# Seven block products in three feed-forwards: weight sums on VectorE, down products in small groups between the pairs

## The chip, the cores and the metric

The kernel runs on one core of a Trainium2 chip. The core has TensorE (PE in the profile) for matrix products, which writes to PSUM, eight banks of 128 x 512 numbers; VectorE (DVE) and ScalarE (ACT), which work on PSUM and on the on-chip memory SBUF; SyncE (SP), which here only issues the DMA transfers; and GpSimd (POOL), which this kernel hardly uses. The engines run their own queues of instructions in order and wait for each other with semaphores. The metric is the time of one execution on the device in microseconds.

## What is computed

Three layers in a row, on 528 rows (16 learned and 512 given) of width 1024, in 32-bit floats: a mixer and a feed-forward, a second mixer and a feed-forward, and then a third mixer and feed-forward on the 512 given rows. The change touches the feed-forwards alone:

```python
def conv_ffn(h, w_up, w_gate, conv_w, conv_b, w_down):      # layers 1 and 2
    u = h @ w_up                                            # 1024 -> 2816
    g = h @ w_gate
    g = lax.conv_general_dilated(g, conv_w...) + conv_b     # 3 taps along the rows, each column alone
    return (jax.nn.silu(g) * u) @ w_down                    # 2816 -> 1024
...
h = h + conv_ffn(rmsnorm(h, norm_ffn[l]), ...)
...
act = silu(rms_norm(x) @ w_gate) * (rms_norm(x) @ w_up)     # layer 3, no convolution
x = x + act @ w_down
```

## The kernel before

**Layout.** Numbers are kept transposed: `hT[k]` holds 128 of the 1024 columns on the partitions and the 528 rows along the free side. The hidden width 2816 is 22 tiles `f` of 128. A weight tile is `[128, 1024]`: the 8 blocks of 128 x 128 that one output tile needs.

**Precision.** Each 32-bit operand is split in two rounded halves, high and low (`w_hi`, `w_lo` of a weight; `xh`, `xl` of the layer's input; `ah`, `al` of the activations), and a product is three matmuls: high by high, high by low, low by high. The high half is a cast, and the low half a subtraction on VectorE. In `split` the cast is recorded by `O.copy`, which the planner may put on ScalarE or VectorE; a plain `SC.copy` stays on ScalarE.

**The first two feed-forwards** are `ffn(0, 1)` and `ffn(1, 3)`, called ffn0 and ffn1 below. For each `f`, `gate_up(f)` multiplies the gate tile over all eight `k`, `8 x 3` matmuls for each range of columns (two of 264 in ffn0; two of 258 in ffn1), reads the banks with the row scale `r` into `g`, runs the convolution as one ScalarE and two VectorE passes into `y`, takes the silu, multiplies the up tile (two ranges of 264; in ffn1 one of 512) into `y` and splits it into `ah`, `al`. `down(gi)` multiplies the down weights of a group of `f` (`GROUPS`: 8, 8 and 6 of them) for the eight output tiles `m`, and adds each bank to `hT[m]`. It stands in the program behind the first `f` of the next group.

**The third feed-forward** (`block2_ffn`, ffn2 below) does without the convolution, on 512 columns. From `f = FS = 2` on it multiplies gate and up together, as a 2 x 2 matrix of blocks by Winograd's seven products instead of eight (`gate_up_fast`). The halves of a weight pair are summed on VectorE into `s13` and `s24` and split there and on ScalarE (`weights`); the sums of the input (`th`, `tl`) are made once. Each product is 4 blocks x 3 matmuls on 256 columns. `sp` and `sv` hold intermediate sums read from the banks, `u` the up result.

**What sets the order.** Every operation is recorded, and at the end of a stage `flush` plans it: a list scheduler with a cost for each instruction, a rank for each stage (`RANK`) and the true dependences, those of reused buffers among them. Weights are recorded with a priority 500 places earlier (`O.shift -= 500`). What it emits is fixed; on the chip each engine takes its own list in order. The profile names one line, L493, for all of it, since one helper emits every instruction; so the rows are told apart by tile names. Weight buffers: three each of `w_raw`, `w_hi`, `w_lo`, and in ffn2 two more of each (`s_raw`, `s_hi`, `s_lo`), taken round by `Ring`. PSUM banks are `d` (three), `at` (four) and `pv` (one); `AllBanks` deals out `d` and `at`.

Of the kernel before, what the change touches and what calls it, by code (L numbers as in the profile page):

```python
# [11 lines left out]
F32 = mybir.dt.float32  # L12
# [16 lines left out]
GROUPS = ((0, 8), (8, 16), (16, 22))  # L29
# [14 lines left out]
FS = 2  # L44
HS = S // 2
# [144 lines left out]
def prepare(i):  # L190
# [23 lines left out]
    for n, (f0, f1) in enumerate(GROUPS):  # L214
# [370 lines left out]
def body(ctx: ExitStack, tc, A, out):  # L585
# [18 lines left out]
    class AllBanks:  # L604
# [514 lines left out]

    def ffn(l, n):  # L1120
# [6 lines left out]
        with ExitStack() as es:  # L1127
# [600 lines left out]
    def block2_ffn():  # L1728
        with ExitStack() as es:
# [6 lines left out]
            class Ring:  # L1736


                def __init__(self, dt, *places):
                    self.dt, self.places, self.n = dt, places, 0  # L1740

                def tile(self):
                    pl, name, bufs = self.places[self.n % len(self.places)]
                    self.n += 1
                    return pl.tile([P, D], self.dt, name=name, bufs=bufs)

            ring = lambda dt, a, b: Ring(dt, *((wp, a, 3), (fp, b, 2)) * 2, (wp, a, 3))
            raws, his, los = ring(F32, "w_raw", "s_raw"), ring(F32R, "w_hi", "s_hi"), ring(F32R, "w_lo", "s_lo")

            def early(fn):  # L1750
                O.shift -= 500
                v = fn()
                O.shift += 500
                return v

            def halves(raw, hi=None, lo=None):

                n = raw.shape[1]
                hi = his.tile()[:, :n] if hi is None else hi
                lo = los.tile()[:, :n] if lo is None else lo  # L1760
# [125 lines left out]
```

## Time and profile before

| | us |
|---|---|
| median of 3 runs | 2363.95 (2362.64 to 2364.92) |
| the profiled execution | 2365.07 |
| its span, first to last instruction | 2362.9 |
| TensorE busy in the span | 2334.1 (99%) |
| VectorE busy | 1793.0 (76%) |
| ScalarE busy | 968.3 (41%) |

Busy time is the time that an engine's records cover. Records of one engine may overlap, so that their durations add up to more than the busy time. A row of groups gives the operation, what it writes and reads, its shape and its count; then the time that the group covers and the mean of one record; then the time that the engine stood idle before these instructions, and what ended it. TensorE's matmul records overlap most, and the time of one in a row is best read from a stretch with nothing else in it, as the stretch's time by the count.

### The profile page before, as it was taken

The numbers are of one execution on the slowest core, as the hardware profiler recorded it, in microseconds if no ns is written. First come the engines' busy times: TensorE is split into PE (matmuls) and PEld (weight loads), VectorE is DVE, ScalarE is ACT, GpSimd is POOL, SyncE is SP. The second block draws the span as 40 slices with busy tenths as digits, with TensorE's granted clock in tenths as the row PEclk, the third lists the DMA queues.
The fourth block names the chain that finished last, engine by engine and source line by source line (L and its number), as shares of the span: only waits on it lengthen the run. The fifth ranks groups of instructions, "written<-read, shape, count | busy, mean of one in ns | idle before, by whom it ended". The sixth has DMA issues, their size and how long they took to land.

```text
span 2362.9 us, 38568 instructions
## 1 busy us (share of the span) xinstructions
PE 2334.1 (99%) x15488; PEld 2125.5 (90%) x15488; DVE 1793.0 (76%) x3512; ACT 968.3 (41%) x1842; POOL 0.2 (0%) x4
## 2 busy tenths in 40 slices
PE   7999999999999999999999999999999999999999
PEld 7999999999999999999888888877888888889998
DVE  6999898764655779997665647876898877987965
ACT  4423556310111278885211203344677613443422
POOL 0000000000000000000000000000000000000000
PEclk9999999999999999999999999999999999999999
DMA  5222221322222211103223223322222122332322
GB/s 200 70 72 70 73 84 57 111 92 90 90 90 88 93 64 55 55 25 102 90 90 100 90 90 97 122 70 86 82 90 72 53 95 89 102 122 80 126 77 84
DMA packets 66546, 205.98 MB, mean 87 GB/s; under 512 B 7972, under 2 KB 14576, under 8 KB 66368
## 3 DMA queue, kind: packets, MB, share of 16 engines
q1 hardware_dynamic: 66368, 203.53, 27.1%
q8 instruction: 121, 1.98, 0.4%
q14 instruction: 57, 0.47, 0.1%
HBM read 201.37 MB, written 6.84 MB: 88 GB/s over the span
## 4 chain that ended last, share of the span: by engine, by line
PE 94%; DVE 3%; DMA 2%; issue 1%; ACT 1%; SPq 0%; DVEq 0%; ACTq 0%
PE d L493 54%; PE at L493 37%; PE pv L493 2%; DMA w_raw<-w_even 1%; DVE w_lo L493 1%; DVE s_lo L493 1%; DVE w_raw L493 0%; DMA w_raw<-w_gs 0%; DVE g L493 0%; DMA h<-h 0%; ACT w_hi L493 0%; DMA ob<-c_oh 0%; DVE sqh L493 0%; DVE s_raw L493 0%; SPq L493 0%
## 5 line engine op out<-in xcount | busy, mean ns | idle before, releaser
L493 PE MATMUL d<-xh,w_hi 128*128 128x264 f32 (+5 forms) x2082 | 616.2, 318 | 8.1 <-ACT w_hi L493 8.0
L493 PE MATMUL d<-xl,w_hi 128*128 128x264 f32 (+5 forms) x2082 | 618.4, 319 | 1.1 <-DVE xl L493 1.0
L493 PE MATMUL d<-xh,w_lo 128*128 128x264 f32 (+5 forms) x2082 | 614.0, 318 | 0.0
L493 DVE TENSOR_TENSOR w_lo<-w_raw,w_hi 128x1024 fp32r<-128x1024 f32 (+4 forms) x363 | 401.1, 1107 | 53.2 <-PE d L493 18.4
L493 PEld LDWEIGHTS d<-xh,w_hi 128*128 128x128 f32 x2082 | 377.4, 189 | 36.3 <-ACT w_hi L493 8.0
L493 PEld LDWEIGHTS d<-xl,w_hi 128*128 128x128 f32 x2082 | 377.3, 189 | 25.9 <-DVE xl L493 2.3
L493 PEld LDWEIGHTS d<-xh,w_lo 128*128 128x128 f32 x2082 | 376.3, 189 | 26.6 <-issue 1.9
L493 ACT CAST w_hi<-w_raw 128x1024 fp32r<-128x1024 f32 (+5 forms) x181 | 172.8, 955 | 328.2 <-PE d L493 230.5
L493 DVE CAST w_hi<-w_raw 128x1024 fp32r<-128x1024 f32 (+4 forms) x182 | 116.4, 640 | 188.0 <-PE d L493 113.0
L493 PE MATMUL at<-xh,w_hi 128*128 128x264 f32 (+3 forms) x822 | 240.1, 302 | 1.2 <-DVE h L493 1.2
L493 PE MATMUL at<-xh,w_lo 128*128 128x264 f32 (+3 forms) x822 | 240.1, 302 | 0.0
L493 PE MATMUL at<-xl,w_hi 128*128 128x264 f32 (+3 forms) x822 | 240.1, 302 | 0.0
L493 ACT ACTIVATE y<-g,cp 128x528 f32<-128x528 f32 (+1 forms) x44 | 36.2, 824 | 345.6 <-DVE g L493 345.6
L493 PEld LDWEIGHTS at<-xh,w_hi 128*128 128x128 f32 x822 | 152.8, 189 | 7.5 <-issue 1.6
L493 PEld LDWEIGHTS at<-xh,w_lo 128*128 128x128 f32 x822 | 152.8, 189 | 5.4
L493 PEld LDWEIGHTS at<-xl,w_hi 128*128 128x128 f32 x822 | 152.6, 189 | 5.2
L493 PE MATMUL at<-ah,w_lo 128*128 128x264 f32 (+1 forms) x350 | 113.0, 331 | 0.0
L493 PE MATMUL at<-ah,w_hi 128*128 128x264 f32 (+1 forms) x350 | 113.0, 332 | 0.0
L493 PE MATMUL at<-al,w_hi 128*128 128x264 f32 (+1 forms) x350 | 112.9, 332 | 0.0
L493 PE MATMUL d<-ah,w_hi 128*128 128x264 f32 (+1 forms) x274 | 91.1, 333 | 0.0
L493 PE MATMUL d<-al,w_hi 128*128 128x264 f32 (+1 forms) x274 | 91.0, 332 | 0.0
L493 PE MATMUL d<-ah,w_lo 128*128 128x264 f32 (+1 forms) x274 | 90.7, 332 | 0.0
(604 smaller groups left out, 4849.9 us busy)
## 6 DMA issues: line engine op xcount, KB each, us to landing
w_raw<-w_gu SPq DMA_DIRECT2D x92, 512.0 KB, 3.7
w_raw<-w SPq DMA_DIRECT2D x59, 512.0 KB, 3.6
w_raw<-w_dn SPq DMA_DIRECT2D x42, 512.0 KB, 3.8
w_raw<-w_even SPq DMA_DIRECT2D x41, 512.0 KB, 3.8
w_raw<-w_gs SPq DMA_DIRECT2D x25, 512.0 KB, 3.6
w_raw<-w_odd SPq DMA_DIRECT2D x24, 512.0 KB, 3.5
w_raw<-w_dn SPq DMA_DIRECT2D x21, 384.0 KB, 3.1
s_raw<-w_gs SPq DMA_DIRECT2D x15, 512.0 KB, 3.6
```

Source lines behind the costliest of these rows:

```text
L493: return f(*[r(x) for x in a], **{n: r(x) for n, x in k.items()})
```

## The change

Winograd's seven products, which only ffn2 had, are moved into a class `Fast` that all three feed-forwards use. In ffn0 and ffn1 the first two `f` stay as they were, `WHOLE` names three more (6, 11, 16) that keep all eight products (their weights come from the paired tiles through `Fast.tile`), and 17 `f` go through `Fast.pair`. Since two halves of 264 or 258 columns do not fit one bank there, a pair takes four banks in ffn0 and ffn1, three in ffn2. All casts of the weights in `Fast` are `SC.copy`. The convolution is unchanged, and `y` is then multiplied by `u`. Down groups become 4, 4, 4, 4, 3, 3 tiles in ffn0 and ffn1 and 5, 5, 5, 4, 3 in ffn2, and the eight `m` of a group are spread over the `f` of the next one. Buffers: `y` 3 to 2, `ah` and `al` 10 to 8 in ffn0 and ffn1; the halves of the seventh weight block (`s_hi2`, `s_lo2`) one each there, two in ffn2. `AllBanks` deals out `pv` too.

```diff
-GROUPS = ((0, 8), (8, 16), (16, 22))
+GROUPS = ((0, 4), (4, 8), (8, 12), (12, 16), (16, 19), (19, 22))
+GROUPS2 = ((0, 5), (5, 10), (10, 15), (15, 19), (19, 22))
+WHOLE = ((6, 11, 16), (6, 11, 16), ())
...
-            return (pd, pp, pd, pp, pd, pp, pp)[AllBanks.turn % 7].tile(shape, dt, name=("d", "at", "d", "at", "d", "at", "at")[AllBanks.turn % 7])
+            pl, place = ((pd, "d"), (pp, "at"), (pd, "d"), (pp, "at"), (pd, "d"), (pp, "at"), (pp, "at"), (pq, "pv"))[AllBanks.turn % 8]
+            return pl.tile(shape, dt, name=place)
...
+        def halves(self, raw, hi=None, lo=None):
...
+            SC.copy(hi, raw)
+            V.tensor_tensor(lo, raw, hi.bitcast(F32), op=ALU.subtract)
...
+        def blocks(self, f):
+            i = f - FS
+            r1, r2 = self.load(A[self.name][2 * i]), self.load(A[self.name][2 * i + 1])
+            s13, s24 = self.raws.tile(), self.raws.tile()
+            two = lambda t: t.rearrange("p (a b) -> p a b", a=2)
+            V.tensor_tensor(two(s13), two(r2)[:, 0:1, :].to_broadcast([P, 2, 512]), two(r1), op=ALU.add)
+            V.tensor_tensor(s24[:, :512], s13[:, :512], r1[:, 512:], op=ALU.add)
+            V.tensor_tensor(s24[:, 512:], s24[:, :512], r2[:, 512:], op=ALU.add)
+            w1, w24, w13 = self.halves(r1), self.halves(s24), self.halves(s13)
+            a12 = self.halves(r2[:, 512:], *(self.fp.tile([P, 512], F32R, name=n, bufs=self.small_bufs) for n in ("s_hi2", "s_lo2")))
+            part = lambda w, i: tuple(v[:, 4 * i:4 * i + 4, :] for v in w)
+            return part(w1, 1), a12, part(w1, 0), part(w13, 0), part(w24, 0), part(w13, 1), part(w24, 1)
...
+        def pair(self, f, g, u, r):
...
+            self.times(c11, a11, self.b[0][0], True)
+            SC.copy(p, c11)
+            self.times(q, s2, self.t[1], True)
+            self.times(q2, s3, self.t[2], True)
+            V.tensor_tensor(v, q, p, op=ALU.subtract)
+            V.tensor_tensor(p, q2, v, op=ALU.add)
+            self.times(s_, s1, self.t[0], True)
+            V.tensor_tensor(u[:, w:2 * w], p, s_, op=ALU.subtract)
+            self.times(c11, a12, self.b[1][0], False)
+            V.tensor_tensor(g[:, :w], c11, r[:, :w], op=ALU.mult)
+            self.times(q2, a22, self.t[3], False)
+            V.tensor_tensor(u[:, :w], q2, v, op=ALU.add)
+            self.times(s_, s4, self.b[1][1], False)
+            V.tensor_tensor(v, s_, v, op=ALU.subtract)
+            V.tensor_tensor(g[:, w:2 * w], v, r[:, w:2 * w], op=ALU.mult)
...
             def gate_up(f):
                 g = fp.tile([P, gw + 2], F32, name="g")
                 V.memset(g[:, 0:2], 0.0)
-                proj(pall, wtile(f"w_gu{l}", 2 * f), x, times(g[:, 2:], r), grange)
-                y = fp.tile([P, uw], F32, name="y", bufs=3)
+                if f < FS:
+                    proj(pall, wtile(f"w_gu{l}", 2 * f), x, times(g[:, 2:], r), grange)
+                elif f in WHOLE[l]:
+                    fast.tile(f, 0, times(g[:, 2:], r), x, grange)
+                else:
+                    u = fp.tile([P, gw], F32, name="u", bufs=1)
+                    fast.pair(f, g[:, 2:], u, r)
+                y = fp.tile([P, uw], F32, name="y", bufs=2)
...
-                proj(pall, wtile(f"w_gu{l}", 2 * f + 1), xu, times(y, y), urange)
-                acts[f] = split_new(y, fp, "ah", "al", 10, uw)
...
+                else:
+                    V.tensor_tensor(y, u[:, o:], y, op=ALU.mult)
+                acts[f] = split_new(y, fp, "ah", "al", 8, uw)
...
-                for m in range(KD):
-                    proj(pall, wtile(f"w_dn{l}_{gi}", m, f1 - f0), a, add_h(m, u0), urange)
-                    if gi == 2:
+                for m in ms:
+                    w = early(lambda: fast.halves(fast.load(A[f"w_dn{l}_{gi}"][m])))
+                    proj(pall, w, a, add_h(m, u0), urange)
+                    if last:
                         add(m)
 
             for gi, (f0, f1) in enumerate(GROUPS):
                 for f in range(f0, f1):
                     gate_up(f)
-                    if gi and f == f0:
-                        down(gi - 1)
-            down(2)
+                    if gi:
+                        down(gi - 1, range(KD * (f - f0) // (f1 - f0), KD * (f + 1 - f0) // (f1 - f0)))
+            down(len(GROUPS) - 1, range(KD))
```

The change of ffn2's loop is the same, with `GROUPS2`.

**Where instructions move: VectorE in the middle of ffn0.** `sv`, `sp`, `u` and `g` are results read from banks; `h` the residual; `rrow` the row scale; the rest are weights. Before:

```order
L493 TENSOR_TENSOR g_0_6807<-at_2_7417,rrow_0_5749 128x264
L493 CAST w_hi_1_7482<-w_raw_2_7323 128x1024
L493 TENSOR_TENSOR g_0_6807<-d_0_7438,rrow_0_5749 128x264
L493 TENSOR_TENSOR w_lo_1_7494<-w_raw_2_7323,w_hi_1_7482 128x1024
L493 SCALAR_TENSOR_TENSOR y_1_7497<-g_0_6807,cp_0_5658,y_1_7497 128x528 x2
L493 MEMSET g_0_7527 128x2
L493 TENSOR_TENSOR y_1_7497<-y_1_7497,rrow_0_5749 128x528
L493 TENSOR_TENSOR y_1_7497<-at_3_7480,y_1_7497 128x264
L493 CAST w_hi_2_7550<-w_raw_0_7384 128x1024
L493 TENSOR_TENSOR w_lo_2_7559<-w_raw_0_7384,w_hi_2_7550 128x1024
```

After, the same kind of place, with a down product's bank reads, weight sums and bank reads of a pair:

```order
L496 TENSOR_TENSOR h1_0_119<-pv_0_8894,h1_0_119 128x264
L496 TENSOR_TENSOR h1_0_119<-d_1_8911,h1_0_119 128x264
L496 TENSOR_TENSOR w_lo_2_8946<-s_raw_1_8776,w_hi_2_8937 128x512
L496 TENSOR_TENSOR w_raw_0_8954<-s_raw_0_8897,w_raw_2_8875 128x1024
L496 TENSOR_TENSOR s_raw_1_8971<-w_raw_0_8954,w_raw_2_8875 128x512
L496 TENSOR_TENSOR s_raw_1_8971<-s_raw_1_8971,s_raw_0_8897 128x512
L496 TENSOR_TENSOR sv_0_8986<-d_2_8950,sp_0_8961 128x264
L496 TENSOR_TENSOR sp_0_8961<-d_0_8966,sv_0_8986 128x264
L496 TENSOR_TENSOR u_0_9006<-sp_0_8961,at_2_8984 128x264
L496 TENSOR_TENSOR w_lo_1_9017<-s_raw_1_8971,w_hi_1_9003 128x1024
L496 TENSOR_TENSOR g_1_8808<-at_1_8934,rrow_0_5814 128x264
L496 TENSOR_TENSOR s_lo2_0_9039<-s_raw_0_8897,s_hi2_0_9028 128x512
```

The casts are gone from VectorE's list, sums of raw weights have come into it, and the reads of a pair's banks stand between the weights of the next one and of the down product.

**TensorE in the middle of ffn0**, a change of tile before (`xh`, `xl` are halves of the input):

```order
L493 MATMUL d_2_7372<-xh_0_5613,w_hi_0_7239 128x264
L493 MATMUL d_2_7372<-xl_0_5626,w_hi_0_7239 128x264
L493 MATMUL d_2_7372<-xh_0_5613,w_lo_0_7248 128x264
L493 MATMUL d_2_7372<-xh_1_5635,w_hi_0_7239 128x264
L493 MATMUL d_2_7372<-xl_1_5641,w_hi_0_7239 128x264
L493 MATMUL at_2_7417<-xh_2_5340,w_hi_1_7296 128x264
L493 MATMUL at_2_7417<-xl_2_5371,w_hi_1_7296 128x264
L493 MATMUL at_2_7417<-xh_2_5340,w_lo_1_7308 128x264
```

After, the end of a pair's last product and the beginning of a down tile (`ah`, `al` are activations):

```order
L496 MATMUL at_2_8984<-xh_7_5557,w_hi_0_8863 128x264
L496 MATMUL at_2_8984<-xl_7_5573,w_hi_0_8863 128x264
L496 MATMUL at_2_8984<-xh_7_5557,w_lo_0_8880 128x264
L496 MATMUL at_2_8984<-xh_0_5613,w_hi_0_8863 128x264
L496 MATMUL at_2_8984<-xl_0_5626,w_hi_0_8863 128x264
L496 MATMUL at_3_9050<-ah_4_8179,s_hi_0_8899 128x264
L496 MATMUL at_2_8984<-xh_0_5613,w_lo_0_8880 128x264
L496 MATMUL at_3_9050<-al_4_8193,s_hi_0_8899 128x264
L496 MATMUL at_2_8984<-xh_1_5635,w_hi_0_8863 128x264
```

Where a gate tile followed an up tile, a down tile now begins while the pair's last product still runs, in another bank.

**TensorE in ffn2**, from one pair to the next before:

```order
L493 MATMUL at_2_23165<-xh_1_21697,w_hi_0_23013 128x256
L493 MATMUL at_2_23165<-xl_1_21701,w_hi_0_23013 128x256
L493 MATMUL at_2_23165<-xh_1_21697,w_lo_0_23031 128x256
L493 MATMUL d_1_23230<-xh_2_21455,w_hi_1_23084 128x256
L493 MATMUL d_1_23230<-xl_2_21466,w_hi_1_23084 128x256
L493 MATMUL d_1_23230<-xh_2_21455,w_lo_1_23093 128x256
L493 MATMUL d_1_23230<-xh_3_21489,w_hi_1_23084 128x256
```

After, at the end of a pair:

```order
L496 MATMUL at_0_24375<-xh_1_23013,s_hi_1_24271 128x256
L496 MATMUL at_0_24375<-xl_1_23017,s_hi_1_24271 128x256
L496 MATMUL at_0_24375<-xh_1_23013,s_lo_1_24289 128x256
L496 MATMUL at_1_24449<-ah_0_23251,w_hi_1_24292 128x512
L496 MATMUL at_1_24449<-al_0_23266,w_hi_1_24292 128x512
L496 MATMUL at_1_24449<-ah_0_23251,w_lo_1_24300 128x512
L496 MATMUL at_1_24449<-ah_1_23398,w_hi_1_24292 128x512
```

Where the next pair's first product stood behind a pair's last, a down tile of 512 columns now stands.

## Rows read from the trace of the kernel before

**Rows 1.** which engines the chain that ended last goes through
```profile
PE 94%; DVE 3%; DMA 2%; issue 1%; ACT 1%; SPq 0%; DVEq 0%; ACTq 0%
```

**Rows 2.** busy time by stretch (columns: the second line), one row a stage
```profile
core 0: us, PE busy (x) PEld busy (x) DVE busy (x) ACT busy (x) POOL busy (x), PEclk, DMA share, GB/s
440.00:829.00 389.00, 389.00 (x3186) 388.54 (x3185) 243.20 (x393) 70.31 (x94) 0.00 (x0) 1.00 0.29 90
829.00:1117.00 288.00, 286.38 (x2232) 274.51 (x2232) 250.71 (x577) 230.11 (x576) 0.00 (x0) 1.00 0.19 60
1117.00:1494.00 377.00, 377.00 (x2136) 329.88 (x2134) 239.35 (x356) 72.16 (x99) 0.00 (x0) 1.00 0.29 94
2004.00:2363.00 359.00, 346.99 (x2305) 317.73 (x2303) 280.79 (x427) 136.35 (x178) 0.00 (x0) 0.99 0.30 99
```

**Rows 3.** the same view, stretches of 264, 512 and 256 columns only
```profile
450.00:800.00 350.00, 350.00 (x2867) 350.00 (x2866) 214.81 (x344) 55.75 (x72) 0.00 (x0) 1.00 0.28 88
1350.00:1375.00 25.00, 25.00 (x110) 20.47 (x109) 13.75 (x19) 2.40 (x3) 0.00 (x0) 1.00 0.28 89
2150.00:2175.00 25.00, 25.00 (x213) 25.00 (x213) 21.01 (x33) 10.88 (x15) 0.00 (x0) 1.00 0.32 104
```

**Rows 4.** the same view, pieces of the third feed-forward
```profile
2004.00:2060.00 56.00, 53.36 (x363) 48.81 (x362) 53.73 (x86) 29.09 (x41) 0.00 (x0) 1.00 0.36 113
2060.00:2360.00 300.00, 293.63 (x1944) 268.92 (x1943) 227.05 (x342) 107.26 (x137) 0.00 (x0) 0.99 0.30 96
2010.00:2100.00 90.00, 84.96 (x636) 80.45 (x635) 86.03 (x132) 43.37 (x57) 0.00 (x0) 1.00 0.37 121
2180.00:2220.00 40.00, 37.28 (x299) 36.87 (x298) 37.90 (x60) 17.07 (x23) 0.00 (x0) 0.96 0.32 106
2200.00:2220.00 20.00, 19.69 (x153) 19.69 (x154) 18.76 (x31) 8.87 (x12) 0.00 (x0) 0.91 0.33 105
2272.00:2322.00 50.00, 49.56 (x403) 48.70 (x402) 40.52 (x64) 20.00 (x27) 0.00 (x0) 1.00 0.33 101
```

**Rows 5.** TensorE's waits there: us in total, times, longest us
```profile
PE at L493 <- DVE sp L493: 4.3, 3, 2.3
...
PE d L493 <- DVE sp L493: 1.5, 1, 1.5
...
PE d L493 <- DVE w_lo L493: 1.3, 3, 0.4
```

**Rows 6.** VectorE's groups by line in ffn0: xcount, busy us, mean ns, idle before
```profile
L493 DVE TENSOR_TENSOR w_lo<-w_raw,w_hi 128x1024 fp32r<-128x1024 f32 x60 | 73.2, 1220 | 3.4 <-PE at L493 1.7 <-PE d L493 0.8
...
L493 DVE SCALAR_TENSOR_TENSOR y<-g,cp,y 128x528 f32<-128x528 f32 x44 | 33.7, 766 | 1.7 <-ACT y L493 0.9
...
L493 DVE CAST w_hi<-w_raw 128x1024 fp32r<-128x1024 f32 x45 | 31.2, 694 | 36.7 <-PE at L493 19.9 <-PE d L493 16.8
...
L493 DVE TENSOR_TENSOR al<-y,ah 128x528 fp32r<-128x528 f32 x22 | 15.5, 703 | 0.2
...
L493 DVE TENSOR_TENSOR h<-at,h 128x264 f32<-128x264 f32 x27 | 11.6, 430 | 23.2 <-PE at L493 23.1
...
L493 DVE CAST w_hi<-w_raw 128x768 fp32r<-128x768 f32 x6 | 3.4, 560 | 3.9 <-PE at L493 3.1 <-PE d L493 0.8
```

**Rows 7.** the same view, VectorE in the third feed-forward
```profile
L493 DVE TENSOR_TENSOR s_lo<-w_raw,s_hi 128x512 fp32r<-128x512 f32 x13 | 8.9, 686 | 0.0
...
L493 DVE TENSOR_TENSOR w_raw<-s_raw,w_raw 128x1024 f32<-128x1024 f32 x7 | 8.5, 1218 | 0.7 <-DMA w_raw<-w_gs 0.7
```

**Rows 8.** VectorE in order of time: start us, us, what
```profile
2157.63 1.22 DVE L493 TENSOR_TENSOR w_lo<-s_raw,w_hi 128x1024 fp32r<-128x1024 f32 x1
2158.76 0.69 DVE L493 TENSOR_TENSOR s_raw<-s_raw,w_raw 128x512 f32<-128x512 f32 x1
2159.37 0.42 DVE L493 TENSOR_TENSOR g<-sv,rrow 128x256 f32<-128x256 f32 x1
```

**Rows 9.** ScalarE's groups by line in the third feed-forward
```profile
L493 ACT CAST w_hi<-w_raw 128x1024 fp32r<-128x1024 f32 x26 | 27.3, 1052 | 48.8 <-PE at L493 19.0 <-DVE w_raw L493 12.5 <-PE d L493 11.4
```

More of the change, by code (lines that the diff above doesn't have):

```diff
@@ L1734, in block2_ffn @@
             acts = {}
[L1736 to L1748, printed above, removed]
@@ L1788, in block2_ffn @@
-            tx = [[(h[:, j, :], l[:, j, :]) for h, l in ts] for j in range(4)]
-            bx = lambda i, j: [(x[0][k][:, HS * j:HS * j + HS], x[1][k][:, HS * j:HS * j + HS]) for k in range(4 * i, 4 * i + 4)]
-            def times3(ps, w, xs, first):
-                wh, wl = w
-                for k, (xh, xl) in enumerate(xs):
-                    for i, (a, b) in enumerate(((wh, xh), (wh, xl), (wl, xh))):
-                        T.matmul(ps, a[:, k, :], b, start=first and k == 0 and i == 0, stop=k == 3 and i == 2,
-                                 skip_group_check=True)
@@ L1798, in bank @@
-            def bank():
-                return pall.tile([P, 512], F32, name="d")
-            def weights(f):
-                r1, r2 = load("w_gs2", 2 * (f - FS)), load("w_gs2", 2 * (f - FS) + 1)
-                s13, s24 = raws.tile(), raws.tile()
-                two = lambda t: t.rearrange("p (a b) -> p a b", a=2)
-                V.tensor_tensor(two(s13), two(r2)[:, 0:1, :].to_broadcast([P, 2, 512]), two(r1), op=ALU.add)
-                V.tensor_tensor(s24[:, :512], s13[:, :512], r1[:, 512:], op=ALU.add)
-                V.tensor_tensor(s24[:, 512:], s24[:, :512], r2[:, 512:], op=ALU.add)
-                w1, w24, w13 = halves(r1), halves(s24), halves(s13)
-                a12 = halves(r2[:, 512:], *(fp.tile([P, 512], F32R, name=n, bufs=2) for n in ("s_hi2", "s_lo2")))
-                part = lambda w, i: tuple(v[:, 4 * i:4 * i + 4, :] for v in w)
-                return part(w1, 1), a12, part(w1, 0), part(w13, 0), part(w24, 0), part(w13, 1), part(w24, 1)
@@ L1838, in gate_up_fast, with gate_up @@
+            fast = Fast(fp, "w_gs2", lambda k: gcol(6, k), NM, HS, 2)
+            def gate_up(f):
+                g = fp.tile([P, S], F32, name="g2", bufs=2)
+                if f < FS:
+                    proj(pall, wtile("w_gu2", 2 * f), x, times(g, r), ONE)
+                else:
+                    u = fp.tile([P, S], F32, name="u2", bufs=2)
+                    fast.pair(f, g, u, r)
                 SC.activation(g, g, AF.Silu)
                 V.tensor_tensor(g, g, r, op=ALU.mult)
-                V.tensor_tensor(g, u, g, op=ALU.mult)
+                if f < FS:
+                    proj(pall, wtile("w_gu2", 2 * f + 1), x, times(g, g), ONE)
+                else:
+                    V.tensor_tensor(g, u, g, op=ALU.mult)
@@ L1853, in down @@
-            def down(gi):
-                f0, f1 = GROUPS[gi]
-                n = (f1 - f0) * P
+            def down(gi, ms):
+                f0, f1 = GROUPS2[gi]
                 a = [acts[f][0] for f in range(f0, f1)], [acts[f][1] for f in range(f0, f1)]
-                for m in range(KD):
-                    w = early(lambda: halves(load(f"w_dn2_{gi}", m, n)))
+                for m in ms:
+                    w = early(lambda: fast.halves(fast.load(A[f"w_dn2_{gi}"][m])))
                     proj(pall, w, a, add_h(m, NM), ONE)
-                    if gi == 2:
+                    if gi == len(GROUPS2) - 1:
@@ L1861, in down @@
                         dma(out[P * m:P * m + P, :], hT[m][:, NM:])
-            for gi, (f0, f1) in enumerate(GROUPS):
+            for gi, (f0, f1) in enumerate(GROUPS2):
                 for f in range(f0, f1):
                     gate_up(f)
-                    if gi and f == f0:
-                        down(gi - 1)
-            down(2)
+                    if gi:
+                        down(gi - 1, range(KD * (f - f0) // (f1 - f0), KD * (f + 1 - f0) // (f1 - f0)))
+            down(len(GROUPS2) - 1, range(KD))
```

153 lines of the change are left out of this document (84 added, 69 removed).

## The prediction

> **What bounds the kernel now.** First the chain of waits: 94% of what ended last is TensorE itself [rows 1]. So the time changes with what TensorE has to do and with how long it stands still, and every other engine counts only where it makes TensorE stand. Then the table by stage [rows 2]: in the two long feed-forwards (ffn0 at 440 to 829 us, ffn1 at 1117 to 1494) TensorE has no idle time at all, with VectorE busy 63%. The odd mixer between them, VectorE busy 87%, leaves TensorE idle 1.62 of 288 us, 0.6%. The third feed-forward (ffn2, from 2004 us) already multiplies in seven block products. There TensorE is idle 12.0 of 359 us, 3.0 of them after 2360 us, in the output's tail.
>
> Third, ffn2 in pieces [rows 4]. In 2010 to 2100, nearly all pairs of tiles without a down product, VectorE is busy 96% and TensorE idle 5.0 us (5.6%). In 2180 to 2220, pairs again, it is 95% and 2.7 us (6.8%). In 2272 to 2322 it is 81% and 0.44 us (0.9%). The waits name the releaser: most of TensorE's waiting is for `sp`, the VectorE pass that reads a product's bank before the next product may go on there [rows 5]. This is the measure for the change: what TensorE loses against VectorE's busy share.
>
> **The change, part by part.** *Matmuls taken away.* A feed-forward tile pair (gate and up of one f) was 96 matmuls of 264 columns in ffn0; seven products of 4 x 3 make 84. A matmul of 264 costs 350/2867 = 0.122 us [rows 3]. Of 22 f, 2 stay as they were and 3 stay whole, so 17 change: 17 x 12 x 0.122 = **-24.9 us**, from 387.7 to 362.8 us of matmuls. In ffn1 an f was 48 of 258 and 24 of 512 columns; now it is 84 of 258. 512 columns take 25/109 = 0.229 us, 256 columns 25/212 = 0.118 [rows 3] (records cut by an edge left out), so 258 about 0.1195. 17 x (48 x 0.1195 + 24 x 0.229 - 84 x 0.1195) = **-20.4 us**, 369.3 to 348.9. ffn2 has the matmuls it had. TensorE stood on the path throughout in ffn0 and ffn1, so these 45.3 us come off the path, less what it newly waits.
>
> *VectorE's work.* In ffn0, by mean durations [rows 6, 7]: a pair gains three weight sums (1.22 + 2 x 0.685 = 2.6 us), 1.9 us of low halves (3 x 1.22 + 0.69 against 2 x 1.22), three more bank reads (1.3) and the product of u and y (0.7): 6.5 us, times 17 = 110. The sums of the input add 24 passes, 13 us, once. Six down groups instead of three add 48 bank reads at 0.43 = 21 us and 4 us of smaller splits. What goes: 51 casts of weights (31.2 + 3.4 us) and some of activations (2), which ScalarE now does. All in all the records grow from 256 to 366 us in 587 instructions; the same list at ffn1's widths gives 251 to 360 in 542.
>
> Those are records, and records overlap: a pass of 1.22 us starts at 2157.63 and the next at 2158.76, that one is recorded with 0.69 us and the next starts 0.61 later [rows 8]. Each costs 0.08 to 0.09 us less than its record where the queue is full: 366 - 587 x 0.083 = 317 us for ffn0, 315 for ffn1. The Trainium skill, "VectorE: DVE Perf Modes", section "The DRAIN you can't avoid", says that the next operation does not start until the pipe is empty. The trace agrees about a start-to-start gap but puts it below the record's length. Were whole records to add up, VectorE would be the longer engine, and ffn0 and ffn1 would shrink to 366 and 360 us, 31 us in all, instead of by 45.
>
> So VectorE covers 317 to 347 us of ffn0's 363 (the upper end by ffn0's overlap now, 256 against 243.2 over 393 records [rows 2]), 88 to 96%, and 315 to 342 of ffn1's 349, 90 to 98%. No stretch of this trace has those shares for this long. The nearest rows on either side are the odd mixer (87%, TensorE idle 0.6%) and 2180 to 2220 (95%, 6.8%) [rows 2, 4]. I take 3%, a little below the middle, because the orders put two down tiles behind most pairs, whose work on VectorE is light, where the lossy stretches of ffn2 have none. That is **+10.9 us** in ffn0 (2.2 to 24.7) and **+10.5** in ffn1 (2.1 to 23.7). The early pairs of each stage, which still have no down product beside them, are inside these figures.
>
> *ScalarE.* It takes the casts: 51 x 1.05 us [rows 9] and those of the sums. With 70 us now [rows 2], its records in ffn0 come to some 165 us against 363, no bound. It costs nothing unless a cast is late; that is the third rival.
>
> *Loads.* The weights are as many bytes. Down tiles come smaller and 24 more of them a stage; SyncE only queues them, and DMA is busy 30% there [rows 2]. Cover: the loads are issued a pair ahead, through five places. Nothing.
>
> *Last down group.* It shrinks from six f to three. In ffn1 VectorE then has about 22 us (8 splits, 8 bank reads and the next norm's 22 passes) beside 16.5 us of matmuls. The next stage's first three tiles are already loaded and need no norm, 16 us of matmuls, so I take nothing; bound 0 to 5.9 us.
>
> *ffn2.* Its pairs now alternate with one or two down tiles. Till 2060 nothing changes, 2.6 us idle [rows 4], since no down group is ready before. Of the 6.4 us lost in 2060 to 2360, some 2.5 should stay and 4 go: 13 us of records more (34 instructions, 16 more bank reads among them) bring VectorE from 281 us [rows 2] to 281 to 303 of 343, 82 to 88%, but evenly, and at 81 to 87% the loss was 0.6 to 0.9%. In 2200 to 2220 the granted clock is 0.91 [rows 4], so some 3.6 us at 1.2 instead of 2.4 GHz, behind the waits of that stretch: 1.8 us, of which I count 1.5. **-5.5 us** (-9 to 0).
>
> *Sum:* -24.9 + 10.9 - 20.4 + 10.5 - 5.5 = -29.4 us on the profiled execution's 2365.1 us (span 2362.9): 2335.7. The median of the runs shown lies 1.1 us below that execution, hence **2334**. With all terms at their good ends -50, at their bad ends +3 (+9 with the last group's).
>
> **Rivals.** *VectorE costs nothing* (chance 0.20). The planner spreads the passes so well that TensorE idles 0.6% in ffn0 and ffn1: -22.7 - 18.3 - 9 = -50, 2313 us; the case is 2311 to 2322. For it: at 81% and 87% TensorE lost under 1%. Against: in 2010 to 2100 VectorE had 4 of 90 us free, and TensorE lost 5.6%.
>
> *VectorE is the bound* (0.18). The loss of 2180 to 2220 holds all through, 6.8%: -0.2 + 3.3 - 2 = +1, 2365; the case is 2346 to 2368. For it: the last three pairs of ffn0 and ffn1 have 2.7 down tiles of four k-tiles or three beside them, at the end more passes for the same matmuls, so that VectorE needs 93 to 95% of TensorE's time even with full overlap. Against: the whole tiles at 6, 11 and 16, each with about 8 us of free VectorE.
>
> *The weights come too late* (0.06, slower). High and low halves have five places each. A pair takes three of them, the two down tiles behind it the other two, so the next pair's first half can be made only when the sixth product of this pair has been multiplied. The chain is a cast (1.05 [rows 9]) and a low half (1.22), 2.3 us. Uncovered in all 34 pairs it costs 78 us, 2412. It decides from 29.4/34 = 0.9 us a pair. Against: the seventh product (1.5 us) and two down tiles (5.9) stand between, and ffn2 shows waits for `w_lo` or `s_lo` of 0.4 us at most. For: behind the down tile's passes VectorE's queue may be long.
>
> *The clock falls* (0.04, slower). A spell like the one in 2200 to 2220 costs 1.8 us; ffn2 has one in its 20 pairs. One in each of the 34 new pairs costs 61 us, 2395; from 16 on the gain is gone. The Trainium skill, "TensorE: Matmul & The Clock Gate", section "A second HAM failure mode: psum-queue depth-cycling", tells of such a case: short idle times between matmul groups that cycle through the banks make the clock swing. The new code does cycle through all eight banks; the trace shows one fall only, where idle time gathered.
>
> **How the numbers follow.** Forecast 2322 to 2346, chance 0.52, with the rivals 0.20, 0.18, 0.06, 0.04. About 0.2% (4.7 us) is what a measurement of this kernel can tell from no change. Faster by more: 0.52 + 0.20 + 0.11 of the second rival = 0.83. Within: the rest of that rival, 0.07. Slower: 0.10. The range 2312 to 2358 holds the forecast, nearly all of the first rival and half of the second, about 0.80.
>
> **What would show it.** ffn0 should last 370 to 378 us instead of 389 and ffn1 355 to 364 instead of 377, with VectorE busy near 90% and TensorE idle 2 to 4%, the waits for VectorE's `sp`, `w_lo` or `s_lo`. A ffn2 still idle by 6 us or more after its first 60 would refute its term. Idle under 1% makes the first rival right. Waits for `w_hi`, `s_hi` of ScalarE in every pair, or a clock under 0.97 over a stage, make one of the last two right. Mixers that change by over 2 us would make the whole frame wrong.

## The result, and the profile after

| | before | after |
|---|---|---|
| median, us (4 runs each) | 2364.06 (2362.64 to 2364.92) | 2342.97 (2341.8 to 2345.48) |
| after by before | | 0.9913 (95% interval 0.9896 to 0.9930) |
| span of the profiled execution, us | 2362.9 | 2340.4 |

The kernel became 21.1 us faster. 2334 was forecast, so 9 us of the expected gain are missing. The page of the kernel after, busy times and the chain of waits by engine (before: the table above and [rows 1]):

```profile
PE 2291.1 (98%) x15488; PEld 2095.9 (90%) x15488; DVE 1976.9 (84%) x3923; ACT 1171.0 (50%) x2160; POOL 0.2 (0%) x4
...
PE 93%; DVE 3%; DMA 2%; ACT 1%; issue 1%; SPq 0%; ACTq 0%; DVEq 0%
```

TensorE still sets the time and has 43 us less to do. Now the stages, kernel after, in the view of [rows 2] and [rows 4] (stretch, its length, busy time and record count of PE, PEld, DVE, ACT, POOL, then PEclk, DMA share, GB/s). Everything starts earlier here: ffn0 at 438 us, ffn1 at 1099, ffn2 at 1992.

```profile
438.00:812.00 374.00, 368.05 (x3003) 366.07 (x3003) 331.51 (x588) 168.68 (x239) 0.00 (x0) 1.00 0.30 98
469.00:514.00 45.00, 40.70 (x325) 39.60 (x324) 40.60 (x77) 19.45 (x27) 0.00 (x0) 1.00 0.28 90
520.00:790.00 270.00, 270.00 (x2218) 270.00 (x2218) 236.70 (x413) 113.14 (x157) 0.00 (x0) 1.00 0.29 95
1099.00:1468.00 369.00, 351.48 (x2308) 320.76 (x2307) 326.14 (x545) 169.06 (x246) 0.00 (x0) 0.99 0.31 99
1129.00:1159.00 30.00, 25.52 (x189) 23.76 (x189) 28.16 (x47) 13.32 (x20) 0.00 (x0) 1.00 0.24 69
1165.00:1440.00 275.00, 275.00 (x1808) 252.04 (x1807) 238.26 (x393) 116.17 (x165) 0.00 (x0) 1.00 0.30 97
1455.00:1470.00 15.00, 0.00 (x0) 0.00 (x0) 13.51 (x22) 7.56 (x13) 0.00 (x0) 0.64 0.16 45
1992.00:2048.00 56.00, 54.52 (x374) 49.99 (x373) 54.02 (x89) 29.97 (x45) 0.00 (x0) 1.00 0.34 110
2048.00:2338.00 290.00, 288.76 (x1931) 265.08 (x1930) 236.69 (x372) 111.15 (x154) 0.00 (x0) 1.00 0.31 100
```

Three things are to be seen. In the long middles of ffn0 and ffn1 (third and sixth row) TensorE is never idle, though VectorE is busy 88% and 87%. What is lost in those stages lies near their beginnings (second and fifth row: 4.3 of 45 us and 4.5 of 30). And TensorE does nothing at all for 15 us at the end of ffn1 (seventh row), while VectorE works.

What TensorE waits for in the fifth row (us in total, times, longest):

```profile
PE d L496 <- DVE s_lo L496: 1.7, 1, 1.7
PE d L496 <- ACT w_hi L496: 1.6, 1, 1.6
PE d L496 <- DVE w_lo L496: 1.2, 1, 1.2
```

All of it is for halves of weights, one of them a cast of ScalarE. In the second row 1.0 us is for `s_lo`, and most of the rest for passes that read a pair's banks (`u` 2.4 us on VectorE, `sp` 0.9 on ScalarE). The first down product starts on TensorE at 492.9 us in ffn0 and at 1144.3 in ffn1; all but the last wait of each row (1.6 and 1.7 us) lies ahead of it.

**The stop.** TensorE in order of time there, kernel after (start us, us, what, and in brackets the idle time ahead of it with its releaser):

```profile
1454.33 0.63 PE L496 MATMUL d<-xh,w_hi 128*128 128x512 f32 x2
1470.48 1.43 PE L496 MATMUL at<-qsa,rb 32*8 32x383 f32 x2 [15.52 <-DMA rb<-rb]
1471.84 0.80 PE L496 MATMUL d<-xh,w_hi 128*128 128x512 f32 x1
...
1475.42 0.63 PE L496 MATMUL d<-xh,w_lo 128*128 128x512 f32 x1
1475.85 0.63 PE L496 MATMUL d<-xh,w_hi 128*128 128x512 f32 x1
...
1478.42 0.39 PE L496 MATMUL d<-xl,w_hi 128*128 128x512 f32 x1
1478.65 0.40 PE L496 MATMUL d<-xh,w_lo 128*128 128x512 f32 x1
```

The instruction that waits is a tiny matmul of the third mixer's relative-bias table, a 32 x 8 table `rb` by a one-hot matrix in `qsa`. In the order after, it is third in the new stage's list for TensorE. Before, the trace has 58 projection matmuls and 16 short ones of the norm between the last down product and it (15 us), and it waited for nothing. It needs a load. The queue that issues loads, SyncE's, kernel after:

```profile
1457.01 0.43 SPq L496 DMA_DIRECT2D hgain<-hgain  x1
1467.99 0.33 SPq L496 DMA_DIRECT2D yo<-c_fsel  x1
...
1468.75 0.41 SPq L496 DMA_DIRECT2D rb<-rb  x1
```

And what that queue waited for (us in total, times, longest), with VectorE's end of the stage in order of time:

```profile
SPq L496 <- DVE acc L496: 10.5, 1, 10.5
```

```profile
1466.63 0.68 DVE L496 TENSOR_TENSOR rrow<-rrow,y 128x512 f32<-128x512 f32 x1
1467.23 0.68 DVE L496 TENSOR_TENSOR acc<-acc,y 128x512 f32<-128x512 f32 x1
1467.86 0.06 DVE L496 MEMSET vr<- 128x2 f32 x1
```

So the chain is this. `yo` takes a place in SBUF that the norm's last VectorE pass still reads (`acc<-acc,y`, done at 1467.9). Its load waits 10.5 us at the head of SyncE's queue, `rb` stands two places behind it, the table matmul waits for `rb`, and behind it in TensorE's queue stand three tiles of projection matmuls that need neither that load nor the norm's result, only `xh` and `xl` of the new input and a bank. VectorE itself ends 13 us after TensorE's last matmul. The stop has a tail: in 1460 to 1474 us the granted clock is 0.50 (1.2 GHz instead of 2.4), and eleven matmuls after it start some 0.43 us apart (1475.42, 1475.85) instead of 0.23 (1478.42, 1478.65), some 2.3 us. The clock, columns as above:

```profile
1460.00:1464.00 4.00, 0.00 (x0) 0.00 (x0) 4.00 (x7) 1.85 (x3) 0.00 (x0) 0.50 0.00 0
1464.00:1470.00 6.00, 0.00 (x0) 0.00 (x0) 4.89 (x10) 1.85 (x3) 0.00 (x0) 0.50 0.09 21
1470.00:1474.00 4.00, 3.52 (x7) 1.89 (x8) 0.00 (x0) 1.39 (x3) 0.00 (x0) 0.50 0.11 24
```

### The profile page after: what moved, and what is told of

Same layout as the page of the kernel before. It is cut to its first block, busy times and chain, and to the rows that moved or that the text cites. A ratio compares the mean times of both kernels' runs of the same rounds, so it can differ in the third digit from the quotient of the medians.

```text
span 2340.4 us, 39716 instructions
## 1 busy us (share of the span) xinstructions
PE 2291.1 (98%) x15488; PEld 2095.9 (90%) x15488; DVE 1976.9 (84%) x3923; ACT 1171.0 (50%) x2160; POOL 0.2 (0%) x4
## 4 chain that ended last, share of the span: by engine, by line
PE 93%; DVE 3%; DMA 2%; ACT 1%; issue 1%; SPq 0%; ACTq 0%; DVEq 0%
PE d L496 52%; PE at L496 33%; PE pv L496 8%; DMA w_raw<-w_even 1%; DVE w_lo L496 1%; DVE w_raw L496 0%; DVE s_lo L496 0%; DVE xl L496 0%; ACT w_hi L496 0%; DMA h<-h 0%; DVE y L496 0%; DMA ob<-c_oh 0%; DVE acc L496 0%; DMA s_raw<-w_gs 0%; DVE g L496 0%
## 5 line engine op out<-in xcount | busy, mean ns | idle before, releaser
L496 PE MATMUL d<-xh,w_hi 128*128 128x264 f32 (+5 forms) x1668 | 494.0, 323 | 10.4 <-ACT w_hi L496 8.2
L496 PE MATMUL d<-xl,w_hi 128*128 128x264 f32 (+5 forms) x1668 | 495.6, 324 | 1.3 <-DVE xl L496 1.3
L496 PE MATMUL d<-xh,w_lo 128*128 128x264 f32 (+5 forms) x1668 | 491.0, 322 | 0.0
L496 DVE TENSOR_TENSOR w_lo<-w_raw,w_hi 128x1024 fp32r<-128x1024 f32 (+5 forms) x328 | 331.8, 1015 | 55.4 <-ACT w_hi L496 40.6
L496 ACT CAST s_hi<-w_raw 128x512 fp32r<-128x512 f32 (+3 forms) x98 | 77.4, 794 | 85.7 <-PE at L496 38.6
L496 PE MATMUL at<-xh,w_hi 128*128 128x264 f32 (+3 forms) x332 | 96.8, 296 | 2.3 <-DVE u L496 1.6
L496 PE MATMUL at<-xh,w_lo 128*128 128x264 f32 (+3 forms) x332 | 97.1, 296 | 0.0
L496 PE MATMUL at<-xl,w_hi 128*128 128x264 f32 (+3 forms) x332 | 96.7, 296 | 0.0
L496 DVE TENSOR_TENSOR s_lo<-w_raw,s_hi 128x512 fp32r<-128x512 f32 (+3 forms) x98 | 87.9, 902 | 6.3 <-ACT s_hi L496 5.3
L496 PE MATMUL at<-xh,s_hi 128*128 128x264 f32 (+3 forms) x272 | 77.7, 285 | 1.2 <-ACT sp L496 1.2
```

Source lines behind the costliest of these rows:

```text
L496: return f(*[r(x) for x in a], **{n: r(x) for n, x in k.items()})
```

## Experiments on the stop

Where nothing else is said, a kernel below is compared with the kernel after, which ran on another occasion. The kernel before, run beside each of them, took 2363.7 to 2365.0 us, so differences of about a microsecond say nothing.

**The table loaded early.** Both operands of the table matmul get a place of their own, loaded before ffn1.

```diff
-            oh = unit("qsa", p=32)[:, :383]
-            dma(oh, A["c_oh2"])
-            rb = const("rb2", [32, 8], pl=bc)
...
-            T.matmul(ps[:8, :383], rb, oh, start=True, stop=True)
+            T.matmul(ps[:8, :383], tab["rb"], tab["oh"], start=True, stop=True)
...
+        if n == 3:
+            tp = O.pool(ts, "tab")
+            tab["oh"], tab["rb"] = const("c_oh2", [32, 383], pl=tp), const("rb2", [32, 8], pl=tp)
```

> The changed kernel, but the 32 x 383 table of the last mixer and its 32 x 8 factor are loaded before ffn1, into a place of their own, so that the first matmul of that mixer waits for no transfer. Theory 1 (TensorE stood 15.5 us at the end of ffn1 because that matmul stands ahead of the projections in its queue and waits for a transfer that SyncE can issue only after VectorE's last pass over a buffer that is reused): TensorE stands 3 to 6 us there instead of 15.5, in short pieces while it follows VectorE's low halves, and the clock does not fall for long: 12 to 16 us less than the changed kernel's 2343, so 2327 to 2331. Theory 2 (VectorE's tail itself is the cause: the first projections need the low halves of the new input, which are as late): TensorE waits for xl until about 12 us after its last matmul, and the time falls by 4 us at most, to 2339 or more.

Measured: 2337.24 us (2336.64 to 2338.14), 5.7 less than after, between the two expectations. TensorE there:

```profile
1465.19 1.44 PE L496 MATMUL at<-c_oh,rb 32*8 32x383 f32 x2 [9.82 <-DVE h L496]
```

The load was 5.7 us of the stop. With it gone, the same matmul waits for the PSUM bank it writes, which VectorE still has to read for the residual `h`. One wait had hidden a second, of 9.8 us.

**The table matmul put later.** It is recorded behind the third mixer's first three projections and takes a `d` bank.

```diff
-            ps = pp.tile([P, 512], F32, name="at")
-            T.matmul(ps[:8, :383], rb, oh, start=True, stop=True)
...
+                if p == 0:
+                    ps = pd.tile([P, 512], F32, name="d")
+                    T.matmul(ps[:8, :383], rb, oh, start=True, stop=True)
```

> The changed kernel, but the table's small matmul of the last mixer is recorded after the mixer's first three projections and writes to a bank that the first of them has used, so that it stands behind them in TensorE's queue. With the transfer gone (e1_table) it still waited 9.8 us, then for a bank that VectorE reads last. Theory 1 (it is the place at the head of the queue, whatever it waits for): the projections start as soon as VectorE has written their first low half, and TensorE's stop is 2 to 5 us, in pieces; 2327 to 2332. Theory 2 (VectorE's tail holds the projections too): a stop of 9 us or more, now for xl or a bank, and 2336 or more.

Measured: 2332.39 us (2331.56 to 2334.66), 10.6 less than after and just above the range of the first expectation. TensorE's waits for a bank that VectorE reads for `h`, this kernel; the one of 6.1 us is at the end of ffn1:

```profile
PE d L496 <- DVE h L496: 7.4, 3, 6.1
```

So the queue's order is worth 10.6 us, and 6.1 us of stop remain: the projections themselves need a bank that VectorE's late residual sums hold. That is close to the prediction's bound of 5.9, which was worked out from VectorE's surplus of work and named no bank; it shows only once nothing stands in front of it.

**A last down group of six.** ffn1 alone: 4, 4, 4, 4, 6 tiles, as long a last group as before.

```diff
+GROUPS1 = ((0, 4), (4, 8), (8, 12), (12, 16), (16, 22))
...
-                acts[f] = split_new(y, fp, "ah", "al", 8, uw)
+                acts[f] = split_new(y, fp, "ah", "al", 10 if l else 8, uw)
```

> The changed kernel, but ffn1's down groups are 4, 4, 4, 4 and 6, so that the last one has 33 us of matmuls instead of 16.5 to cover VectorE's last passes (and ten places for ah and al there). Theory 1a (the stop at the end of ffn1 exists because the last group became too short for VectorE's norm passes): the stop is under 2 us and the clock stays up, 15 to 18 us less, 2325 to 2328. Theory 1b (the position of the table's matmul alone is to blame): SyncE is still held until VectorE's last pass, the stop stays over 10 us, and the time over 2337.

Measured: 2326.58 us (2324.9 to 2327.6), 16.4 less than after, as the first expectation has it. The same stretch (columns as above), and the one wait of TensorE that is left at the end of ffn1, for the norm's result:

```profile
1455.00:1470.00 15.00, 13.41 (x69) 11.01 (x68) 10.02 (x21) 6.05 (x11) 0.00 (x0) 1.00 0.20 55
```

```profile
PE at L497 <- DVE rc L497: 1.6, 1, 1.6
```

With twice the matmuls beside VectorE's tail neither the load nor a bank comes late, and the clock stays up. The three runs agree on one cause: VectorE ends later than TensorE. Through which wait TensorE meets it is the order's doing.

**Few large groups.** Three groups of 7, 7 and 8, each whole behind the next one's first tile, as the kernel before has it.

```diff
-GROUPS = ((0, 4), (4, 8), (8, 12), (12, 16), (16, 19), (19, 22))
+GROUPS = ((0, 7), (7, 14), (14, 22))
...
-                    if gi:
-                        down(gi - 1, range(KD * (f - f0) // (f1 - f0), KD * (f + 1 - f0) // (f1 - f0)))
+                    if gi and f == f0:
+                        down(gi - 1, range(KD))
```

> The changed kernel with ffn0's and ffn1's down products in three groups of 7, 7 and 8, each whole group behind the first tile of the next, as the kernel before has them in 8, 8 and 6. Six pairs in a row then stand without a down product, and there VectorE needs 12.0 us a pair (records overlapping) against TensorE's 10.25 in ffn0 and 11.9 against 10.05 in ffn1. Theory A (the down products between the pairs are what makes VectorE fit): 10 to 20 us more in each stage, less the stop at the end of ffn1 (16 us), which the longer last group covers: 2347 to 2367. Theory B (three whole tiles are enough): 2335 or less.

Measured: 2344.19 us (2342.79 to 2345.24), as long as after, and below the range of the first expectation. (`ah` and `al` have nine places here.) The stop at the end of ffn1 is gone, and its gain is lost again where pairs stand alone (ffn0, columns as above):

```profile
454.00:499.00 45.00, 40.41 (x310) 38.07 (x308) 42.87 (x68) 20.13 (x26) 0.00 (x0) 1.00 0.28 95
619.00:634.00 15.00, 12.40 (x90) 11.91 (x89) 13.66 (x24) 5.78 (x9) 0.00 (x0) 0.90 0.25 84
739.00:754.00 15.00, 13.34 (x101) 12.38 (x101) 13.88 (x25) 6.78 (x9) 0.00 (x0) 1.00 0.22 71
```

VectorE is busy 91 to 95% in these rows, and TensorE stops for 8.9 of their 75 us. In the whole of ffn0 and ffn1 TensorE idles 22 us, where after it is some 10 without the stop, although VectorE's busy time in the execution is 32 us less (1944.9 us). Spreading the down tiles is thus the part of the change that keeps TensorE busy.

## Experiments on VectorE's share

**No whole tiles.** The three `f` of ffn0 and of ffn1 that kept eight products become pairs too.

```diff
-WHOLE = ((6, 11, 16), (6, 11, 16), ())
+WHOLE = ((), (), ())
```

> The changed kernel with no whole tiles: 20 instead of 17 pairs in seven products in ffn0 and ffn1 each. Per tile 12 matmuls of 264 (1.47 us) or the like of 258 and 512 (1.2 us) go: -8.0 us of matmuls in all. Theory A (VectorE keeps up wherever a down product stands beside a pair): all 8 us are gained, 2335, and TensorE's idle time after the first 75 us of each stage stays under 1 us. Theory B (the whole tiles are what lets VectorE catch up): TensorE idles 3% more, 10 us in each stage, and the time is 2343 to 2355.

Measured: 2335.17 us (2332.55 to 2335.98), 7.8 less than after. The number is the expected one, but not for one reason alone: the stop at the end of ffn1 came out at 6.1 us in this order, the first pairs lost more, and behind four short stops of 1.1 to 2.6 us (near 500, 818, 1132 and 1487 us) the granted clock is 0.50 for some 3.4 us each, which it is not in after. What the run shows cleanly is the middle:

```profile
469.00:514.00 45.00, 39.91 (x304) 38.87 (x305) 40.66 (x72) 19.82 (x28) 0.00 (x0) 0.96 0.26 77
520.00:790.00 270.00, 270.00 (x2216) 270.00 (x2215) 249.12 (x443) 119.36 (x167) 0.00 (x0) 1.00 0.30 95
1165.00:1440.00 275.00, 275.00 (x1863) 254.58 (x1862) 254.25 (x423) 124.87 (x178) 0.00 (x0) 1.00 0.31 97
```

VectorE is busy 92% over 270 us, and TensorE waits for nothing. The tiles at 6, 11 and 16 bought no slack that was needed there.

**The whole tiles early.** The same three, at 3, 4 and 5.

```diff
-WHOLE = ((6, 11, 16), (6, 11, 16), ())
+WHOLE = ((3, 4, 5), (3, 4, 5), ())
```

> The changed kernel with the three whole tiles at f = 3, 4, 5 instead of 6, 11, 16. Theory A (what is lost inside ffn0 and ffn1, about 6 and 4.5 us of idle time, all falls in the first 75 us, where pairs have no down product beside them, and nothing later): the early idle time falls to 1 to 2 us a stage and none comes later, 6 to 9 us less, 2334 to 2337. Theory B (the later whole tiles are needed): the early gain is lost again later, 2341 to 2350, with waits for VectorE after the first 75 us.

Measured: 2331.05 us (2330.18 to 2333.61), 11.9 less than after and below the range of the first expectation. The stop at the end of ffn1 was still there, 15.0 us. The first pairs:

```profile
469.00:514.00 45.00, 45.00 (x371) 45.00 (x370) 35.90 (x64) 16.88 (x21) 0.00 (x0) 1.00 0.24 75
...
1129.00:1159.00 30.00, 30.00 (x181) 26.60 (x180) 21.66 (x38) 7.99 (x11) 0.00 (x0) 1.00 0.26 79
```

No idle time is left in either stretch. The gain is a little larger than the 9 us of idle time of these two rows after; where the rest came from was not traced.

**More work for VectorE.** Each pair of ffn0 and ffn1 computes one low half twice, a redundant pass of 128 x 1024 (34 passes, 1.13 us apart: 38 us).

```diff
+            for _ in range(1 if self.small_bufs == 1 else 0):
+                V.tensor_tensor(w13[1].rearrange("p a b -> p (a b)"), s13, w13[0].rearrange("p a b -> p (a b)").bitcast(F32), op=ALU.subtract)
```

> The changed kernel with one more pass of VectorE over 128 x 1024 (1.13 us where the queue is full) in each of the 17 pairs of ffn0 and ffn1, the low half of s13 written twice. VectorE then needs, records overlapping, 95 to 96% of a pair's and its down tiles' time on TensorE in ffn0 and 99% in ffn1. Theory A (VectorE costs only what its work exceeds TensorE's by): the stretches after the first 75 us still lose under 2 us in ffn0 and 2 to 5 in ffn1, the early stretches 4 to 6 us more in all; 2350 to 2356. Theory B (my rate: 3% idle near 91%, 6 to 7% near 95%): idle time of 6% all through, 30 us more, 2370 to 2380.

Measured: 2358.83 us (2356.46 to 2360.27), 15.9 more than after, between the two expectations and nearer the first. The middles, and the beginnings:

```profile
520.00:740.00 220.00, 220.00 (x1807) 220.00 (x1807) 198.31 (x337) 92.11 (x125) 0.00 (x0) 1.00 0.29 95
1180.00:1440.00 260.00, 259.94 (x1715) 238.57 (x1714) 237.12 (x378) 109.99 (x155) 0.00 (x0) 1.00 0.30 98
...
439.00:514.00 75.00, 66.87 (x517) 64.76 (x517) 68.39 (x120) 36.87 (x54) 0.00 (x0) 0.98 0.28 94
1099.00:1159.00 60.00, 56.52 (x402) 53.09 (x402) 56.09 (x99) 34.05 (x53) 0.00 (x0) 0.97 0.26 84
```

The middles took the additional passes without a stop. The cost came where VectorE already had no room: at the beginnings and at the ends of the stages, and in matmuls at 1.2 GHz behind the new stops. (ffn1 starts some 9 us later here; between the last row and the second TensorE waits for `s_lo` twice more, 1.6 and 3.7 us.) So 38 us of VectorE cost 16 us of time, and not evenly. The stop at the end of ffn1 came out at 7.3 and 2.9 us here instead of 15.5; without that luck the cost would be some 5 us higher, an estimate from these waits.

## The third feed-forward alone, and a better kernel

**Only ffn2's groups**, in the kernel before.

```diff
+GROUPS2 = ((0, 5), (5, 10), (10, 15), (15, 19), (19, 22))
...
-                    if gi and f == f0:
-                        down(gi - 1)
+                    if gi:
+                        down(gi - 1, range(KD * (f - f0) // (f1 - f0), KD * (f + 1 - f0) // (f1 - f0)))
```

> The kernel before with one part of the change alone: ffn2's down products in groups of 5, 5, 5, 4, 3, spread between the pairs. The changed kernel's ffn2 lasts 10.1 us less than before (355.2 to 345.1 by VectorE's first and last instruction of the stage). Theory A (that is this part's own doing): 2353 to 2355, TensorE's idle time in ffn2 under 3 us without the output's tail, no fall of the clock in it. Theory B (part of it came from another start of the stage): 2357 or more.

Measured: 2353.97 us (2353.67 to 2354.84), a ratio of 0.9959 (0.9944 to 0.9974) to before, some 10 us, as the first expectation has it. ffn2 in the two pieces of [rows 4]:

```profile
2004.00:2060.00 56.00, 54.93 (x375) 50.09 (x375) 53.34 (x85) 29.74 (x41) 0.00 (x0) 1.00 0.32 108
2060.00:2350.00 290.00, 288.18 (x1928) 264.59 (x1926) 236.15 (x371) 110.74 (x154) 0.00 (x0) 1.00 0.31 101
```

TensorE idles 1.1 and 1.8 us instead of 2.6 and 6.4, and the clock stays at 1.00.

**The two cures together.** ffn1's last group of six, and whole tiles at 3, 4, 5.

```diff
+GROUPS1 = ((0, 4), (4, 8), (8, 12), (12, 16), (16, 22))
-WHOLE = ((6, 11, 16), (6, 11, 16), ())
+WHOLE = ((3, 4, 5), (3, 4, 5), ())
```

> Joins two edits that each ran alone: ffn1's last down groups become one of six tiles, and the whole tiles of ffn0 and ffn1 move from 6, 11, 16 to 3, 4, 5. Theory A (the two losses are separate: a stop at the end of ffn1, and idle time of TensorE in the first pairs of each stage): the gains add, 16.4 + 11.9 us, so 2342.9 - 28.3 = 2314 to 2316 us, no idle time in the first 75 us of either stage, and a stop of under 2 us at the end of ffn1. Theory B (both edits removed the same thing, half-clock spells that any change of the timing shifts): the gains do not add, 2322 to 2330 us.

Measured: 2314.43 us (2314.28 to 2316.23), 28.5 less than after where the two gains add to 28.3. They are separate losses.

With two whole tiles, `WHOLE = ((3, 4), (3, 4), ())`:

> As the last one with tiles 3 and 4 whole, so one more pair in each of ffn0 and ffn1: 1.5 + 1.2 us of matmuls less. Theory A with VectorE's surplus in the first pairs as the cause of their loss: at three whole tiles that loss was gone, at none it was some 8 us a stage; two whole tiles leave 0 to 2 us a stage, so 2312 to 2316 us. Theory B (any VectorE share over 90% costs): over 2317 us.

Measured: 2313.75 us (2312.55 to 2315.88), as the first of the two expected. From the kernel with three it can't be told apart.

With tile 3 alone, `WHOLE = ((3,), (3,), ())`:

> As the last one with tile 3 alone whole: another 2.7 us of matmuls less, 5.3 us less than with three. Theory A: 2 to 5 us of idle time a stage come back in the first pairs, so 2313 to 2319 us: the matmuls saved are about what the first pairs lose again, and the three kernels lie within 5 us of each other. Theory B (any VectorE share over 90% costs): over 2320 us, with idle time in the interleaved stretches too. Theory C (the first pairs' loss hangs on where whole tiles stand, not on how many): as with three whole, no idle time, 2309 to 2311 us.

Measured: **2311.14 us** (2310.79 to 2312.43), 0.9775 of before (0.9759 to 0.9791): 53.9 us faster than before and 31.8 faster than after. Its stretches:

```profile
469.00:514.00 45.00, 45.00 (x372) 45.00 (x371) 41.33 (x76) 20.58 (x28) 0.00 (x0) 1.00 0.30 100
520.00:790.00 270.00, 270.00 (x2216) 269.80 (x2215) 249.88 (x447) 120.62 (x170) 0.00 (x0) 1.00 0.31 98
1129.00:1159.00 30.00, 30.00 (x222) 28.56 (x220) 27.80 (x48) 14.21 (x21) 0.00 (x0) 1.00 0.19 63
1165.00:1440.00 275.00, 272.51 (x1816) 250.32 (x1816) 251.92 (x414) 129.44 (x182) 0.00 (x0) 1.00 0.30 100
```

These stretches of the beginnings lose nothing with one whole tile, so from three down to one the number of whole tiles was not what mattered. By the count of recorded matmuls, TensorE does 2.75 pairs ahead of the first down product in ffn0 and 2 in ffn1 in the kernel after, and 1.75 in both here: one pair fewer there is enough. The third theory of that run (the place, not the number) fits, at the edge of its range. In ffn1's middle 2.5 us come back, at 92% of VectorE, 1.6 of them waits for halves of weights; without whole tiles the same stretch lost none at 92%, so the share alone doesn't tell it. The 270 us of ffn0's middle show no loss.

## Where the prediction held, and where not

The direction and the range held; the time was 9 us too low. That it is not further off is in part luck: terms that were too high and a gain that was too small made up for most of a stop that stood in the sum with nothing. By steps:

- *Matmuls taken away* held. ffn0 lasts from VectorE's first instruction to its last 373.9 us instead of 389.6, inside the 370 to 378 forecast. That is 15.7 less, where 24.9 us of matmuls went, so by these marks 9.2 came back and 10.9 were expected. But TensorE's idle time there is only 5.9 us (first row of stages), with the clock at 1.00. The rest lies in the marks: VectorE's last pass ends 7.3 us behind TensorE's last down product (805.0, 812.3), where before it was 3.4 (825.6, 829.0).
- *VectorE's work*: the list was right. 587 records add up to 365.7 us in ffn0 (366 forecast) and 542 to 359.4 in ffn1 (360), and cover 331.5 and 326.1 us, in the middle of 317 to 347 and 315 to 342. ScalarE's busy 169 us are the 165 forecast. That records overlap, which the prediction weighed against the Trainium skill, "VectorE: DVE Perf Modes", section "The DRAIN you can't avoid", holds in the new code: the pass at 1466.63 is recorded with 0.68 us and the next starts 0.60 us later.
- *3% idle all through* was the wrong form and twice too much: TensorE idles 5.9 us in ffn0 and 4.5 in ffn1 ahead of the stop, where 10.9 and 10.5 were forecast. The prediction took a share between that of two rows of before and spread it over the stage. In the traces the loss is nothing in the middles of the kernel after, at 87 and 88% of VectorE, nothing to 0.9% at 92%, and 10 to 15% in the stretches of the first pairs, most of it ahead of the first down product. The stretches of ffn2 that gave the 5.6 and 6.8% [rows 4] were of this second kind; the prediction had seen that and still averaged. "The early pairs of each stage ... are inside these figures" was the sentence to work out instead.
- *Last down group*, "I take nothing; bound 0 to 5.9 us", failed. It had the cause, VectorE's 22 us beside 16.5 us of matmuls, and the wrong consequence: that TensorE would go on with the next stage's three loaded tiles. The order put a dependent matmul ahead of them, and the stop was 15.5 us with some 2.3 of slow matmuls behind it. Without that matmul in front, the bound would nearly have held (6.1 us). In the profiled executions 6.6 us are missing (2342.3 instead of 2335.7). This step, 17.8 us in all, explains that and more: against it stand the 11 us less of idle time in the two stages and 4.6 more of gain in ffn2. Some 4 us are left that these terms don't explain.
- *ffn2*, -5.5, was too small: 355.2 to 345.1 us in VectorE's marks, and 10 us alone. Idle time of its first 56 us, which was to stay, went from 2.6 to 1.5 us; behind them 6.4 us became 1.2 where some 2.5 were to stay; and the fall of the clock went.
- *Mixers that change by over 2 us*: by VectorE's marks the last mixer grew from 511.2 to 524.5 us and ffn1 shrank by only 8.9, to 368.5, outside the 355 to 364 forecast. The two belong together, 4.3 us longer where 9.9 less were forecast: the mark at VectorE's last pass falls into the stop. The frame was wrong at this one seam, not in the mixers; the odd mixer lasts 287.1 us in both.
- Of the rivals, *VectorE costs nothing* is what the middles show, and the kernel with both cures and as many whole tiles as after, at 2314 us, lies in its 2311 to 2322; the best one, at 2311, has two more pairs a stage. *VectorE is the bound* fell: at 92% at most 0.9% was lost where the down tiles lie between. *The weights come too late*: no wait for `w_hi`, `w_lo` or `s_lo` inside the middles after, but all 4.5 us at the beginning of ffn1 are such waits; the rival was right in form for the first pairs and wrong for the rest. *The clock falls*: PEclk is 1.00 in the middle rows, with all eight banks in turn. So the swing of the Trainium skill, "TensorE: Matmul & The Clock Gate", section "A second HAM failure mode: psum-queue depth-cycling", did not come with the cycling alone; the clock fell where TensorE had stopped.

Over the span: -15.7 in ffn0, +4.3 in ffn1 and the last mixer, -10.1 in ffn2 and -1 in the even mixer make -22.5 us, 2362.9 to 2340.4.

## What to carry to other kernels

Cost a second engine's load by stretch: what it needs beside what the first one does there, pair by pair, at the beginning and the end of a stage above all; a mean share says little. When a stage's last group is made smaller, read in the new order what stands first in the bounding engine's queue behind it, and follow each operand to its load, its place's last reader and its bank's last reader. Removing the wait that the trace names may only show the next one behind it; a cure that gives the bounding engine enough work beside the lagging engine's tail takes nearly all of them.

## What was not expected of the hardware

TensorE ran 270 us without idle time while VectorE, which reads the products' banks and makes the sums and low halves of the weights, was busy 92% (the kernel without whole tiles). A stop of 15.5 us cost more than itself: the granted clock was 0.50 from 1460 to 1474 us and matmuls of 512 columns ran 0.43 us apart instead of 0.23.
